# Token tiles of 128 rows, two features to a bank, two gate jobs first, and other figures in the plan of a hybrid decoder layer

## The chip, the cores and the metric

The kernel runs on one core of a Trainium2 chip. The metric is the device time of one execution in microseconds (us), the median of several runs.

## What is computed

One inference step of one layer of a hybrid decoder, for a prompt of 16 meta tokens and 512 tokens and for 8 sampled sequences of one token each; together they are T = 536 token columns of D_MODEL = 1024 features, all in fp32.

```python
h = rmsnorm(x, norm_mix)
(qa, ka, va, za, ba, aa, qb, kb, vb, rb, lrb, gate_a, gate_b) = split(h @ w_in)
qkv_a = silu(causal_dwconv(concat(qa, ka, va)))       # then l2norm of q and k
o_a, s_a = gated_delta_net(qa, ka, va, g_a, beta_a)   # chunks for the prompt, recurrent for samples
o_b, s_b = gla(qb, kb, vb, lg_b)
o_a = rmsnorm(o_a, onorm_a) * silu(za)
o_b = rmsnorm(o_b, onorm_b) * silu(rb)
mix = sigmoid(gate_a) * (o_a @ w_a_out) + sigmoid(gate_b) * (o_b @ w_b_out)
x = x + mix @ w_o
h = rmsnorm(x, norm_ffn)
u, gf = split(h @ w_ffn_in)
x = x + (gelu(causal_dwconv(u) + b) * gf) @ w_ffn_out
y = rmsnorm(x, norm_final)
```

The states of both recurrences and of both convolutions are outputs as well.

## The kernel before

**Jobs.** Activations lie transposed: 128 features on the partitions, the 536 token columns along the free axis. A job computes 128 output features for a range of columns: for each of 8 feature blocks of 128 (4 or 22 in some), three matmuls of fp32r parts (`wh` with the high part of the activations, `wh` with the low part, `wl` with the high part), each in two halves of the columns, into one of two PSUM buffers `g`. So a job with 8 blocks is 48 matmuls. The weights of a block pair are loaded as `wr`; ScalarE casts them to `wh`, VectorE takes the rest `wl` (GpSimd for the first two jobs). After the last matmul an evacuation function reads `g`.

**Order of the jobs** (`one`, line 1720 on): `z0` to `z3` (the gate of the delta net); the convolution jobs `dj` 4 and 5; the small job (beta, decay, low rank); `dj` 6, 7, 0 to 3, 8 to 11; `kb`, `qb`, `rb`, `vb`; 16 gate jobs (`ga` and `gb`, stored in `z_d`); then `w_a_out` and `w_b_out` in turn, `w_o`, and the FFN. The first nine jobs read the tokens scaled by `norm_mix` only (`xh`, `xl`, from `xact`) and their evacuation multiplies by the row `rx` of inverse norms. The others read the normalised `hTh`, `hTl` (`hact`). `z0` and `z1` form a group that does the first half of the columns of both before the second half of both, so that work can begin with half of the tokens.

**The prologue.** `loads` brings the tokens as `xu`. TensorE first runs 28 fp32 warm-up products (two instructions each). `turn` then transposes: before, tile 4 (16 meta tokens) with tiles 0 and 1 for the first half, tiles 2 and 3 with 8 sampled tokens for the second, feature block by feature block, each into its own PSUM bank (`s`, four banks). ScalarE writes `xh` from the bank, VectorE `xl`, and the raw copy `xr` is made by VectorE and ScalarE in turn. `token_norms` squares each tile on ScalarE, raises to the power -0.5 on GpSimd, has VectorE make a diagonal matrix `dg`, and TensorE multiplies ones with it to spread the norms over all partitions as `rx`. `normalised` then makes `hn`, `hTh`, `hTl` per feature block, and stores `xr` to DRAM as `xT_d` for the residual.

**The recurrences.** `gdn_prep`, `gdn_chain` and the `onorm` of key a work on the delta net once its convolutions are done; `gla_decay`, `gla_prep` (which sets a flag `gat0` to `gat4` after each chunk; `gat0` are the meta tokens), `gla_chain`, `gla_sample` and the `onorm` of key b work on GLA. `gla_sample` loads the eight states `Sg` and reads them with small matmuls (`reads`) that add up in one `s` bank; it waits for `gat4`. All of this is issued beside the jobs.

**The order of instructions** is decided in Python before the program is built. Class `Plan` collects every operation with a priority (its time in a rough model less a lead, set by `ahead`), simulates the engines, the DMA queue and the buffers with a cost per operation, and emits the instructions in the order that the simulation gives. The costs stand in `Engine.__getattr__` (from line 366), `mm` and `tr` (from line 414); `Plan.emit` holds the model of the DMA queue (`bw`) and of latencies. On the chip each engine then takes its instructions in that order.

Of the kernel before, what the change touches and what calls it, by code (L numbers as in the profile page):

```python
# [78 lines left out]


# [37 lines left out]
class Plan:  # L118
# [50 lines left out]
    def emit(self):  # L169
# [38 lines left out]
        while len(done) < len(ops):  # L208
# [54 lines left out]
            for u in op.users:  # L263
                u.left -= 1
                u.need = max(u.need, op.finish - (op.lat if op.eng == u.eng == "PE" else 0.0))
                if u.left == 0:
                    offer(u)
# [92 lines left out]
class Engine:  # L360
# [5 lines left out]
    def __getattr__(self, name):  # L366
        f = getattr(self.eng, name)

        def call(*args, **kw):
# [24 lines left out]
def body(ctx, tc, I, O):  # L394
# [19 lines left out]
    def mm(out, lhsT, rhs, start=True, stop=True):  # L414
        n, m = rhs.shape[-1], lhsT.shape[-1]
        k = lhsT.shape[0]
        small = rhs.dtype != F32R and (m <= 64 or k <= 64)
        if rhs.dtype == F32R:
            cost = max(n / 2400 + .0117, .112 * m / P, .025)
        else:  # L420
            cost = n / 2400 + .005 if m <= 32 or k <= 32 else .058 if m <= 64 and n <= 64 else max(n / 600 + .005, .222 * m / P)
        duty = (n / 2400 if rhs.dtype == F32R else n / 2400 + .007 if m <= 32 else n / 600) * k / P
        drv.matmul(cost, out, [lhsT, rhs], lambda: nc.tensor.matmul(out=out, lhsT=lhsT, rhs=rhs, start=start, stop=stop), duty, small)  # L423

    def tr(out, in_):
        k = in_.shape[0]
        drv.matmul(max(.03, .110 * k / P), out, [in_], lambda: nc.tensor.transpose(out, in_, ident[:k, :k]), 2 * k / 2400 * k / P, k <= 64)  # L427
# [26 lines left out]
    def halves(c0, n):  # L454

        return (0, NMETA + 2 * P - c0), (NMETA + 2 * P - c0, n)
# [41 lines left out]
    def load_raw(src, K, lead=12.0):  # L498
        raw = drv.new("wr", 3, pp.tile([P, 8, P], F32, tag="wr", name="wr", bufs=3))
        with ahead(lead):  # L500
            dma(out=raw[:, :K, :], in_=src.rearrange("(k p) m -> p k m", p=P))
        return raw
# [12 lines left out]
    class Weights:  # L515
# [6 lines left out]
        def first(self, *leads):  # L522

            for lead in leads:
                s, K, j = self.q[self.nr]
                self.raw[self.nr] = load_raw(s, K, drv.t + lead)
                self.nr += 1

        def ahead(self, nr, nw, eng=None):
            while self.nr < min(self.i + nr, len(self.q)):  # L530
                s, K, j = self.q[self.nr]
                self.raw[self.nr] = j.loaded() if j.loaded else load_raw(s, K)
# [100 lines left out]
    def R_(name, dt=F32R):  # L633
# [16 lines left out]
    pool.memset(half, -0.5)  # L650

    W_LEADS = 25.0, 24.0
    loads = [(cst[:, C_ID:C_ID + P], I["cst"][:, C_ID:C_ID + P]), (xts[0][0], I["x_prompt"][0, 0:P, :]),
             (nmr, I["norm_mix"][0].rearrange("(k p) -> k p", p=P)), (xts[4][0], I["meta_tokens"]),
             (xts[1][0], I["x_prompt"][0, P:2 * P, :]), None, None,
             (xts[2][0], I["x_prompt"][0, 2 * P:3 * P, :]), (xts[3][0], I["x_prompt"][0, 3 * P:4 * P, :]),
             (xts[5][0], I["x_sample"][:, 0, :]), (xu[2][NMETA:NMETA + NS, :DM], I["x_sample"][:, 0, :]), (cst[:, P:], I["cst"][:, P:])]
    for n, l in enumerate(loads):
        if l:
            with ahead(30.0 - n):  # L660
                dma(out=l[0], in_=l[1])

# [11 lines left out]
    def turn(tiles, c0, c1):  # L674

        for k in range(8):
            ps = S_()
            for i in tiles:
                xt, c = xts[i]
                tr(ps[:, c - c0:c - c0 + xt.shape[0]], xt[:, k * P:(k + 1) * P])  # L680
            x, hi, lo = (t[k // 4][:, k % 4, c0:c1] for t in (xr, xh, xl))
            pv = ps[:, :c1 - c0]
            act.activation(hi, pv, AF.Copy, scale=nrm_mix[:, k:k + 1])
            stt(lo, pv, nrm_mix[:, k:k + 1], f32(hi), MUL, SUB)
            if k % 2:
                act.copy(x, pv)
            else:
                dve.tensor_copy(x, pv)

    def token_norms(tiles):  # L690

        for i in tiles:

            xt, n = (xts[i][0], P) if i < 4 else (xu[2][:NMETA + NS, :DM], NMETA + NS)
            r = rsx[:n, i:i + 1]
            act.activation(T_("jk")[:n], xt, AF.Square, scale=DM ** -0.5, accum_out=ssx[:n, i:i + 1])
            pool.tensor_scalar_add(r, ssx[:n, i:i + 1], EPS)
            tt(r, r, half[:n], ALU.pow, pool)
            dg = Cc("dg")[:n, :n]
            dve.tensor_scalar_mul(dg, ident[:n, :n], r)  # L700
            ps = S_()
            mm(ps[:, :n], cst[:n, C_SEL + R_ONE:C_SEL + R_ONE + 1].to_broadcast([n, P]), dg)
            for a, b, c in [(0, P, xts[i][1])] if i < 4 else [(0, NMETA, 0), (NMETA, n, TP)]:
                dve.tensor_copy(rx[:, c:c + b - a], ps[:, a:b])

    def normalised():
        for i in range(2):
            dma(out=xT_d[:, 4 * i:4 * i + 4, :], in_=xr[i])
        for k in range(8):
            h = Cc("hn")[:, :T]  # L710
# [56 lines left out]
    def small_evac(ps):  # L767
        sv = Cc("sv")[:96, :T]
        tt(sv, ps, rx[:96], MUL)
# [588 lines left out]
    def gla_sample():  # L1358

        yield from drv.wait("D", "kb3", "qb3", "gdns", "gat4")  # L1360
# [70 lines left out]
    def z_evac(n, norms=None):  # L1431
        def f(ps):
            zt = Z_("zt")[:, :TQ]
            if norms is not None:
                tt(zt, ps, norms[:, Q0:T], MUL)
                act.activation(zt, zt, AF.Silu)
# [283 lines left out]
    one = [wj(OFF_ZA + n * P, Q0, TQ, z_evac(n, rx), acts=xact, halves=n < 2) for n in range(4)]  # L1720
    one += [dj(4, rx, acts=xact), dj(5, rx, acts=xact), Job([(None, 8)], xact, 0, T, small_evac, M=96, loaded=small_raw)]
    one += [dj(m, rx, acts=xact) for m in (6, 7)] + [dj(m) for m in (0, 1, 2, 3, 8, 9, 10, 11)]
# [4 lines left out]
    one += [wj(OFF_GA + n * P, Q0, TQ, z_evac(12 + n)) for n in range(16)]  # L1727
# [98 lines left out]
```

## Time and profile before

| | us |
|---|---|
| median of 3 runs (lowest to highest) | 986.65 (986.44 to 990.56) |
| profiled execution | 986.13 |
| its span | 984.4 |
| TensorE busy | 968.4 (98%) |
| VectorE busy | 606.6 (62%) |
| ScalarE busy | 463.3 (47%) |
| GpSimd busy | 185.3 (19%) |

In the rows PE is TensorE's matmul part and PEld its weight load, DVE is VectorE, ACT is ScalarE, POOL is GpSimd, SP is the engine that issues the DMAs. L389, L423 and L427 are the lines of helpers (every vector operation, every matmul, every transpose), so operations are told apart by the tiles: `out<-in`. Matmuls are pipelined: the distance from one start to the next is what one costs, not its own duration.

### The profile page before, as it was taken

How to read it: one execution, taken by the hardware profiler on the slowest of the kernel's cores; microseconds unless marked ns; L12 is line 12 of the kernel's file. 1: busy time of each engine (PE TensorE's matmuls, PEld its weight loads, DVE VectorE, ACT ScalarE, POOL GpSimd, SP SyncE). 2: the span in 40 equal slices, each digit the busy share in tenths (PEclk: the TensorE clock that was granted, in tenths of full speed). 3: DMA queues.
4: the chain of work that ended last, by engine and by line, in shares of the span. 5: the costliest groups of instructions: out<-in, count | busy, mean ns of one | idle time of the engine just before them, and what ended most of it. 6: DMA issues, size and time to landing. Idle time of an engine off the chain costs nothing.

```text
span 984.4 us, 21968 instructions
## 1 busy us (share of the span) xinstructions
PE 968.4 (98%) x9022; PEld 950.4 (97%) x9022; DVE 606.6 (62%) x1197; ACT 463.3 (47%) x905; POOL 185.3 (19%) x278
## 2 busy tenths in 40 slices
PE   9999999999999999999999999999999999999996
PEld 8999999998999999999999999999999999999996
DVE  4879867883457867324754447777776766433254
ACT  6566654745446455244643337344443433232343
POOL 4100116101222244012211122111122111000000
PEclk9999999999999999999999999999999999999998
DMA  7643322445123232656655536477655554433354
GB/s 235 184 116 88 87 66 65 133 130 142 34 77 87 79 90 83 188 161 204 204 174 150 162 110 182 139 237 213 199 157 156 166 152 126 126 118 93 111 143 140
DMA packets 208681, 135.48 MB, mean 138 GB/s; under 512 B 14353, under 2 KB 196392, under 8 KB 208308
## 3 DMA queue, kind: packets, MB, share of 16 engines
q1 hardware_dynamic: 208580, 134.07, 46.9%
q8 instruction: 71, 1.16, 0.5%
q14 instruction: 30, 0.25, 0.1%
HBM read 112.26 MB, written 21.98 MB: 136 GB/s over the span
## 4 chain that ended last, share of the span: by engine, by line
PE 81%; DMA 1%; issue 0%; DVE 0%; ACT 0%; SPq 0%; POOLq 0%; POOL 0%; ACTq 0%
PE g L423 71%; PE s L423 8%; PE s L427 1%; DMA xb_d<-Xb 0%; DMA NT<-xb_d 0%; PE on L423 0%; ACT zt L389 0%; PE pk L423 0%; SPq L389 0%; PE pq L423 0%; POOLq L1822 0%; ACT gat L389 0%; DVE wy L389 0%; DVE ga L389 0%; POOL rfb L389 0%
## 5 line engine op out<-in xcount | busy, mean ns | idle before, releaser
L389 ACT CAST wh<-wr 128x512 fp32r<-128x512 f32 (+1 forms) x300 | 183.1, 612 | 312.3 <-PE g L423 297.4
L389 DVE TENSOR_TENSOR wl<-wr,wh 128x512 fp32r<-128x512 f32 (+1 forms) x296 | 203.6, 698 | 177.1 <-ACT wh L389 175.4
L423 PE MATMUL g<-hTh,wh 128*128 128x268 f32 (+3 forms) x768 | 160.8, 288 | 1.0 <-ACT zt L389 1.0
L423 PE MATMUL g<-hTl,wh 128*128 128x268 f32 (+3 forms) x768 | 161.7, 288 | 0.0
L423 PE MATMUL g<-hTh,wl 128*128 128x268 f32 (+3 forms) x768 | 160.9, 288 | 0.0
L423 PE MATMUL g<-h2l,wh 128*128 128x260 f32 x704 | 142.8, 284 | 0.0
L423 PE MATMUL g<-h2h,wh 128*128 128x260 f32 x704 | 142.0, 282 | 0.0
L423 PE MATMUL g<-h2h,wl 128*128 128x260 f32 x704 | 142.0, 283 | 0.0
L423 PEld LDWEIGHTS g<-hTh,wh 128*128 128x128 f32 x768 | 120.0, 189 | 3.6 <-issue 1.9
L423 PEld LDWEIGHTS g<-hTl,wh 128*128 128x128 f32 x768 | 120.9, 189 | 1.7 <-issue 1.2
L423 PEld LDWEIGHTS g<-hTh,wl 128*128 128x128 f32 x768 | 119.8, 189 | 1.5 <-issue 1.2
L423 PEld LDWEIGHTS g<-h2h,wl 128*128 128x128 f32 x704 | 109.3, 189 | 0.1
L423 PEld LDWEIGHTS g<-h2h,wh 128*128 128x128 f32 x704 | 108.6, 189 | 0.1
L423 PEld LDWEIGHTS g<-h2l,wh 128*128 128x128 f32 x704 | 108.6, 189 | 0.0
L423 PE MATMUL g<-actl,wh 128*128 128x260 f32 (+2 forms) x352 | 79.3, 284 | 0.0
L423 PE MATMUL g<-acth,wh 128*128 128x260 f32 (+2 forms) x352 | 78.2, 283 | 0.0
L423 PE MATMUL g<-acth,wl 128*128 128x260 f32 (+2 forms) x352 | 77.9, 282 | 0.0
L423 PEld LDWEIGHTS g<-actl,wh 128*128 128x128 f32 x352 | 57.7, 188 | 0.1
L423 PEld LDWEIGHTS g<-acth,wl 128*128 128x128 f32 x352 | 57.3, 188 | 0.0
L423 PEld LDWEIGHTS g<-acth,wh 128*128 128x128 f32 x352 | 57.2, 188 | 0.0
L389 ACT ACT_TABLE_LOAD x34 | 43.6, 1283 | 7.4 <-DVE na L389 3.4
L389 POOL TENSOR_TENSOR E<-kb,E 128x256 f32<-128x256 f32 (+1 forms) x32 | 25.5, 807 | 56.5 <-DVE E L389 31.9
(362 smaller groups left out, 1675.5 us busy)
## 6 DMA issues: line engine op xcount, KB each, us to landing
wr<-in_w_in SPq DMA_DIRECT2D x56, 512.0 KB
wr<-in_w_ffn_in SPq DMA_DIRECT2D x44, 512.0 KB
wr<-in_w_ffn_out SPq DMA_DIRECT2D x20, 512.0 KB
z_d<-zt SPq DMA_DIRECT2D x28, 261.0 KB
Sg<-in_state_gla SPq DMA_DIRECT2D x8, 512.0 KB
wr<-in_w_b_out SPq DMA_DIRECT2D x8, 512.0 KB
wr<-in_w_o SPq DMA_DIRECT2D x8, 512.0 KB
So<-in_state_gla SPq DMA_DIRECT2D x8, 512.0 KB
```

The lines of the kernel that those rows point to most:

```text
L389: self.drv.issue(self.key, cost, out, ins, 2.2 if self.key == "sync" else 0.17, lambda: f(*args, **kw), func, lock)
L423: drv.matmul(cost, out, [lhsT, rhs], lambda: nc.tensor.matmul(out=out, lhsT=lhsT, rhs=rhs, start=start, stop=stop), duty, small)
L427: drv.matmul(max(.03, .110 * k / P), out, [in_], lambda: nc.tensor.transpose(out, in_, ident[:k, :k]), 2 * k / 2400 * k / P, k <= 64)
```

## The change

Tokens are tiled by 128 rows from the first meta token on: five tiles, the last of 16 prompt tokens and 8 samples, and the halves are cut at column 256 (`XH`). `turn` puts `per` feature blocks into a bank, two in the first half and one in the second; in the second half (and for the last bank of the first) ScalarE makes `xr`. `token_norms` works on groups of tiles (0, 1 and 2, 3, 4), squares odd tiles on VectorE, and multiplies the column of norms, spread along the free axis, with the identity instead of ones with a diagonal. `xT_d` is stored block by block. `z0` and `z1` run over all 536 columns. Two gate jobs come fifth and sixth, on `xact`, with `rx` in their evacuation; `dj` 4 to 7 and the small job read `hact`, so their evacuations multiply by no norm. `gla_sample` waits for `gat1`. In the plan, an operation that follows another on the same engine waits for less of its latency (`saved`), the DMA queue starts at 2.8 us and moves 320 instead of 300 (thousand bytes per us), and small matmuls and transposes cost other amounts.

```diff
+    def saved(self, user):
+
+        return 0.0 if user.eng != self.eng or self.eng == "sync" else self.lat - (0.0 if self.eng == "PE" else 0.03)
...
-        self.free, self.hw, self.bw, self.queue, self.set = {}, 0.0, 0.0, [], None
+        self.free, self.hw, self.bw, self.queue, self.set = {}, 0.0, 2.8, [], None
...
-                    op.need = max(op.need, d.finish - (d.lat if d.eng == op.eng == "PE" else 0.0))
+                    op.need = max(op.need, d.finish - d.saved(op))
...
-                cost = n * out[0].shape[0] * max(4 / 300e3, 0.43e-3 / run)
+                cost = n * out[0].shape[0] * max(4 / 320e3, 0.43e-3 / run)
...
-            cost = n / 2400 + .005 if m <= 32 or k <= 32 else .058 if m <= 64 and n <= 64 else max(n / 600 + .005, .222 * m / P)
+            cost = n / 2400 + .005 if m <= 32 else .12 if m <= 64 and n <= 64 else max(n / 600 + .005, .222 * m / P if k > 32 else 0.0)
...
-        drv.matmul(max(.03, .110 * k / P), out, [in_], lambda: nc.tensor.transpose(out, in_, ident[:k, :k]), 2 * k / 2400 * k / P, k <= 64)
+        drv.matmul(max(.05, .110 * k / P), out, [in_], lambda: nc.tensor.transpose(out, in_, ident[:k, :k]), 2 * k / 2400 * k / P, k <= 64)
...
-        return (0, NMETA + 2 * P - c0), (NMETA + 2 * P - c0, n)
+        return (0, XH - c0), (XH - c0, n)
...
-    xts = [(xu[i // 2][:, (i % 2) * DM:(i % 2 + 1) * DM], NMETA + i * P) for i in range(4)]
-    xts += [(xu[2][:NMETA, :DM], 0), (xu[2][:NS, DM:2 * DM], TP)]
-    XH = NMETA + 2 * P
+    xts = [xu[i // 2][:, (i % 2) * DM:(i % 2 + 1) * DM] for i in range(4)] + [xu[2][:T - 4 * P, :DM]]
+    XH = 2 * P
...
+    def turn(tiles, c0, c1, per):
+
+
+        for k0 in range(0, 8, per):
+            ps = S_()[:, :per * (c1 - c0)].rearrange("p (k t) -> p k t", k=per)
+            for k in range(k0, k0 + per):
+                for i in tiles:
+                    n = xts[i].shape[0]
+                    tr(ps[:, k - k0, i * P - c0:i * P - c0 + n], xts[i][:, k * P:(k + 1) * P])
+            for k in range(k0, k0 + per):
+                hi, lo = (t[k // 4][:, k % 4, c0:c1] for t in (xh, xl))
+                act.activation(hi, ps[:, k - k0], AF.Copy, scale=nrm_mix[:, k:k + 1])
+                stt(lo, ps[:, k - k0], nrm_mix[:, k:k + 1], f32(hi), MUL, SUB)
+            x = xr[k0 // 4][:, k0 % 4:k0 % 4 + per, c0:c1]
+            with ahead(16.0):
+                if per == 1 or k0 == 6:
+                    act.copy(x, ps)
+                else:
+                    dve.tensor_copy(x, ps)
+
+    def token_norms(tiles):
+
+        a, b = tiles[0], tiles[-1] + 1
+        for i in tiles:
+            n = xts[i].shape[0]
+            jk, ss = T_("jk")[:n], ssx[:n, i:i + 1]
+            if i % 2:
+                dve.scalar_tensor_tensor(out=jk, in0=xts[i], scalar=1.0 / DM, in1=xts[i], op0=MUL, op1=MUL, accum_out=ss)
+            else:
+                act.activation(jk, xts[i], AF.Square, scale=DM ** -0.5, accum_out=ss)
+        pool.tensor_scalar_add(rsx[:, a:b], ssx[:, a:b], EPS)
+        tt(rsx[:, a:b], rsx[:, a:b], half.to_broadcast([P, b - a]), ALU.pow, pool)
+        ps, c = S_(), a * P
+        for i in tiles:
+            n = xts[i].shape[0]
+            mm(ps[:, i * P - c:i * P - c + n], rsx[:n, i:i + 1].to_broadcast([n, P]), ident[:n, :n])
+        n = min(b * P, T) - c
+        dve.tensor_copy(rx[:, c:c + n], ps[:, :n])
...
-        for i in range(2):
-            dma(out=xT_d[:, 4 * i:4 * i + 4, :], in_=xr[i])
         for k in range(8):
+            dma(out=xT_d[:, k, :], in_=xr[k // 4][:, k % 4, :])
...
-        yield from drv.wait("D", "kb3", "qb3", "gdns", "gat4")
+        yield from drv.wait("D", "kb3", "qb3", "gdns", "gat1")
...
-    one += [dj(4, rx, acts=xact), dj(5, rx, acts=xact), Job([(None, 8)], xact, 0, T, small_evac, M=96, loaded=small_raw)]
-    one += [dj(m, rx, acts=xact) for m in (6, 7)] + [dj(m) for m in (0, 1, 2, 3, 8, 9, 10, 11)]
+    one = [wj(OFF_ZA + n * P, 0 if n < 2 else Q0, T if n < 2 else TQ, z_evac(n, rx), acts=xact, halves=n < 2) for n in range(4)]
+    gate_job = lambda n, norms=None, **kw: wj(OFF_GA + n * P, Q0, TQ, z_evac(12 + n, norms), **kw)
+    one += [gate_job(n, rx, acts=xact) for n in range(2)]
+    ng = 2
+    raw_, own = dict(norms=rx, acts=xact), ()
+    one += [dj(m, **(raw_ if m in own else {})) for m in (4, 5)]
+    one.append(Job([(None, 8)], xact if 's' in own else hact, 0, T, small_evac, M=96, loaded=small_raw))
...
-    one += [wj(OFF_GA + n * P, Q0, TQ, z_evac(12 + n)) for n in range(16)]
+    one += [gate_job(n) for n in range(ng, 16)]
...
-        turn((4, 0, 1), 0, XH)
+        turn((0, 1), 0, XH, 2)
...
-        turn((2, 3, 5), XH, T)
-    with ahead(20.0):
-        token_norms((0, 1, 2, 3, 4))
+        turn((2, 3, 4), XH, T, 1)
+    with ahead(18.0):
+        token_norms((0, 1))
+        token_norms((2, 3, 4))
```

## Rows read from the trace of the kernel before

**Rows 1.** The page: busy times, the chain that ended last, the weight split.

```profile
PE 968.4 (98%) x9022; PEld 950.4 (97%) x9022; DVE 606.6 (62%) x1197; ACT 463.3 (47%) x905; POOL 185.3 (19%) x278
...
PE 81%; DMA 1%; issue 0%; DVE 0%; ACT 0%; SPq 0%; POOLq 0%; POOL 0%; ACTq 0%
...
L389 DVE TENSOR_TENSOR wl<-wr,wh 128x512 fp32r<-128x512 f32 (+1 forms) x296 | 203.6, 698 | 177.1 <-ACT wh L389 175.4
```

**Rows 2.** TensorE's waits: who was waited for, us in total, times, longest.

```profile
PE s L427 <- DVE xr L389: 0.8, 1, 0.8
...
PE g L423 <- DVE zt L389: 0.4, 1, 0.4
```

**Rows 3.** Instructions of the warm-up: duration ns min/median/max, first and last start.

```profile
L423 PE MATMUL warm<-scm x56: 275/275/579, 1.3 to 10.9; 128*128 128x128 f32 x56
```

**Rows 4.** Windows of the start: length, busy (count) per engine, clock, DMA share, GB/s.

```profile
0.00:11.00 11.00, 9.45 (x67) 8.97 (x67) 1.83 (x6) 5.84 (x10) 5.57 (x18) 1.00 0.83 252
...
11.00:31.47 20.47, 19.65 (x160) 18.09 (x160) 14.75 (x38) 16.14 (x36) 8.44 (x16) 1.00 0.74 243
...
31.50:57.00 25.50, 25.14 (x207) 24.96 (x206) 21.53 (x39) 12.22 (x24) 2.90 (x9) 1.00 0.51 130
```

**Rows 5.** TensorE's timeline in the prologue: start us, us, instruction, count.

```profile
11.49 0.88 PE L427 MATMUL s<-cst,xu 16*128 16x16 f32 x6
12.13 0.36 PE L423 MATMUL g<-xh,wh 128*128 128x258 f32 x1
...
15.74 0.38 PE L427 MATMUL s<-cst,xu 128*128 128x128 f32 x2
15.88 0.36 PE L423 MATMUL g<-xl,wh 128*128 128x258 f32 x1
16.08 0.29 PE L423 MATMUL g<-xh,wl 128*128 128x258 f32 x1
```

**Rows 6.** Windows of one 522-wide job, and of two that are 536 wide.

```profile
37.77:43.64 5.87, 5.87 (x48) 5.87 (x49) 4.57 (x7) 3.38 (x7) 0.00 (x0) 1.00 0.63 144
43.64:55.52 11.88, 11.88 (x99) 11.88 (x98) 10.70 (x19) 4.88 (x9) 1.76 (x5) 1.00 0.44 135
```

**Rows 7.** Instructions of the tiles `xr` and `jk` (the squares) on ScalarE.

```profile
L389 ACT COPY xr<-s x8: 378/384/386, 11.2 to 27.0; 128x272 f32<-128x272 f32 x4, 128x264 f32<-128x264 f32 x4
...
L389 ACT ACTIVATE jk<-xu x5: 1054/1058/1082, 5.2 to 25.9; 128x1024 f32<-128x1024 f32 x4, 24x1024 f32<-24x1024 f32 x1
L389 ACT ACTIVATION_READ_ACCUMULATOR jk<-xu x5: 184/187/224, 6.2 to 26.9; 128x1 f32 x4, 24x1 f32 x1
```

**Rows 8.** Instructions of the tiles `hn`, `hTl`, `zt` and `xT_d`.

```profile
L389 DVE SCALAR_TENSOR_TENSOR hn<-xr,vec,rx x8: 767/770/777, 32.5 to 62.9; 128x536 f32<-128x536 f32 x8
L389 DVE TENSOR_TENSOR hTl<-hn,hTh x8: 708/712/718, 35.6 to 69.0; 128x536 fp32r<-128x536 f32 x8
...
L389 DVE TENSOR_TENSOR zt<-g,rx x4: 693/701/704, 29.9 to 46.8; 128x522 f32<-128x522 f32 x4
...
L389 SPq DMA_DIRECT2D xT_d<-xr x2: 332/345/358, 22.2 to 27.4; - x2
```

**Rows 9.** Instructions of the tiles `Sg`, `ob` and `olb`: the GLA line.

```profile
L423 PE MATMUL s<-Sg,zw x64: 379/379/403, 405.4 to 432.9; 128*32 128x256 f32 x64
L389 DVE SCALAR_TENSOR_TENSOR Sg<-Sg,edl,s x16: 471/476/481, 359.6 to 404.0; 128x256 f32<-128x256 f32 x16
...
L389 ACT ACTIVATE osq<-ob x8: 622/630/646, 435.8 to 442.5; 128x522 f32<-128x522 f32 x8
...
L389 DVE TENSOR_TENSOR olb<-zl,ohb x8: 690/703/1564, 465.4 to 485.9; 128x522 fp32r<-128x522 f32 x8
```

**Rows 10.** Windows of the recurrences, and the stretch below full clock.

```profile
200.00:300.00 100.00, 98.18 (x1203) 94.56 (x1202) 56.12 (x138) 48.81 (x81) 17.18 (x26) 0.98 0.35 95
300.00:400.00 100.00, 98.61 (x1362) 94.80 (x1361) 73.58 (x163) 49.51 (x100) 36.89 (x42) 1.00 0.29 84
...
250.00:260.00 10.00, 10.00 (x103) 9.80 (x102) 4.66 (x14) 4.43 (x7) 1.04 (x1) 0.83 0.27 81
```

More of the change, by code (lines that the diff above doesn't have):

```diff
@@ L264, in emit @@
                 u.left -= 1
-                u.need = max(u.need, op.finish - (op.lat if op.eng == u.eng == "PE" else 0.0))
+                u.need = max(u.need, op.finish - op.saved(u))
                 if u.left == 0:
@@ L496, in patient, with load_raw @@
         drv.hold = hold
-    def load_raw(src, K, lead=12.0):
+    def load_raw(src, K, *leads):
         raw = drv.new("wr", 3, pp.tile([P, 8, P], F32, tag="wr", name="wr", bufs=3))
-        with ahead(lead):
-            dma(out=raw[:, :K, :], in_=src.rearrange("(k p) m -> p k m", p=P))
+        n = K // len(leads)
+        for i, lead in enumerate(leads):
+            with ahead(lead):
+                dma(out=raw[:, i * n:(i + 1) * n, :], in_=src[i * n * P:(i + 1) * n * P].rearrange("(k p) m -> p k m", p=P))
         return raw
@@ L522, in first @@
         def first(self, *leads):
-            for lead in leads:
+            for l in leads:
                 s, K, j = self.q[self.nr]
-                self.raw[self.nr] = load_raw(s, K, drv.t + lead)
+                self.raw[self.nr] = load_raw(s, K, *l)
                 self.nr += 1
@@ L650, in body @@
     pool.memset(half, -0.5)
[L652 to L657, printed above, removed]
+    pool.memset(ssx, 1.0)
+    x_p = I["x_prompt"][0]
+    loads = [(cst[:, C_ID:C_ID + P], I["cst"][:, C_ID:C_ID + P]),
+             (nmr, I["norm_mix"][0].rearrange("(k p) -> k p", p=P)),
+             (xts[0][:NMETA], I["meta_tokens"]), (xts[0][NMETA:], x_p[0:P - NMETA]),
+             (xts[1], x_p[1 * P - NMETA:2 * P - NMETA]),
+             None,
+             None,
+             (xts[2], x_p[2 * P - NMETA:3 * P - NMETA]),
+             (xts[3], x_p[3 * P - NMETA:4 * P - NMETA]),
+             (xts[4][:NMETA], x_p[SEQ - NMETA:]), (xts[4][NMETA:], I["x_sample"][:, 0, :])]
+    W_LEADS = [[30.0 - n] for n, l in enumerate(loads) if not l]
     for n, l in enumerate(loads):
@@ L661, in body @@
                 dma(out=l[0], in_=l[1])
+    with ahead(4.0):
+        dma(out=cst[:, P:], in_=I["cst"][:, P:])
     def warm_up():
@@ L672, in turn_weights @@
         dve.tensor_copy(nrm_mix, ps[:, :8])
-    def turn(tiles, c0, c1):
-        for k in range(8):
[L677 to L704, printed above, removed]
@@ L710, in normalised @@
+    def normalised():
+        for k in range(8):
+            dma(out=xT_d[:, k, :], in_=xr[k // 4][:, k % 4, :])
             h = Cc("hn")[:, :T]
@@ L1434, in f @@
             if norms is not None:
-                tt(zt, ps, norms[:, Q0:T], MUL)
-                act.activation(zt, zt, AF.Silu)
+                tt(zt, ps[:, ps.shape[-1] - TQ:], norms[:, Q0:T], MUL)
+                if n < 12:
+                    act.activation(zt, zt, AF.Silu)
             elif n < 12:
@@ L1718, in body @@
     xact = lambda k: (xh[k // 4][:, k % 4, :], xl[k // 4][:, k % 4, :])
-    one = [wj(OFF_ZA + n * P, Q0, TQ, z_evac(n, rx), acts=xact, halves=n < 2) for n in range(4)]
-    one += [dj(4, rx, acts=xact), dj(5, rx, acts=xact), Job([(None, 8)], xact, 0, T, small_evac, M=96, loaded=small_raw)]
-    one += [dj(m, rx, acts=xact) for m in (6, 7)] + [dj(m) for m in (0, 1, 2, 3, 8, 9, 10, 11)]
+    one = [wj(OFF_ZA + n * P, 0 if n < 2 else Q0, T if n < 2 else TQ, z_evac(n, rx), acts=xact, halves=n < 2) for n in range(4)]
[5 more added lines that the diff above has]
+    one.append(Job([(None, 8)], xact if 's' in own else hact, 0, T, small_evac, M=96, loaded=small_raw))
+    for i, m in enumerate((6, 7, 0, 1, 2, 3, 8, 9, 10, 11)):
+        if i in ():
+            one.append(gate_job(ng))
+            ng += 1
+        one.append(dj(m, **(raw_ if m in own else {})))
     one += [wj(OFF_KB + h * P, 0, T, qkb_evac(kb, h, 1.0, f"kb{h}")) for h in range(H)]
```

6 lines of the change are left out of this document (2 added, 4 removed).

## The prediction

> **What bounds the kernel now.** I read the page first: TensorE is busy for 98% of the span and the chain that ended last is almost all PE [rows 1]. Then TensorE's own waits, stage by stage: the largest one after the start is a 0.8 us wait of a transpose for the copy `xr`, then 0.4 us for `zt` [rows 2]. So no other engine is a bound. The span is the sum of what TensorE issues, and a change moves the time only where it takes instructions off TensorE, makes them cheaper, or opens or closes a wait there. The start is full as well: 56 warm-up matmuls run from 1.3 to 10.9 us [rows 3], and the two windows of the prologue are idle for 1.55 us (1.3 of them before the first matmul) and for 0.82 us, at a granted clock of 1.00 [rows 4]. The first weight matmul therefore waits for queued warm-ups and transposes rather than for data, and a transpose saved there is worth its issue time.
>
> The span is 984.4 us, the profiled execution took 986.13 us, the median of the runs is 986.65 us. I work in differences and set them against the median; the 0.5 us between execution and median is within the spread of the runs.
>
> **Part by part.**
>
> *Tiles of 128 rows.* Before, each of 8 features has a 16-row transpose in the first half and an 8-row one in the second; after, only the second half has a small one (24 rows). Eight transposes go. Price: six transposes of two features (four of 128 rows, two of 16) hold the next weight matmul from 11.49 to 12.13, 0.64 us; a pair of 128-row ones takes 15.74 to 15.88, 0.14 us [rows 5]. So the two small ones with their change of shape cost 0.64 - 2 x 0.14 = 0.36, or 0.18 each: 8 x 0.18 = **-1.44 us**. The 24-row tile has the bound of 0.18 too and replaces the 8-row one at no difference.
>
> *Two features to a bank.* The matmul after a run of transposes needs 0.20 us to the next (15.88 to 16.08) [rows 5], where a job of 48 pairs of weight and token columns takes 5.87 us [rows 6], 0.12 us each: 0.08 us a turn. The first half turns 4 times for 8: **-0.32 us**.
>
> *Wait for the bank.* The 0.8 us [rows 2] is a transpose of the second half that waits until VectorE has copied `xr` out. After, the first half needs half as many banks, and in the second half ScalarE does the copies. ScalarE is not fuller for it: it was busy 16.14 of 20.47 us there [rows 4]; it keeps eight copies of 0.38 us and gets one of 512 columns (some 0.7 us, an estimate from 0.38 us for 264 to 272), and gives up one of the three squares that it did in this stretch, 1.06 + 0.19 us [rows 7]. VectorE takes that square and loses its five `dg` and five of its eight copies. I take **-0.8 us**; the ends are -0.8 and +0.8 (the same wait, once more, behind a ScalarE that now does scale and copy in turn).
>
> *Wider first jobs.* `z0` and `z1` run over 536 columns for 522. Two 536-wide jobs take 11.88 us, a 522-wide one 5.87 us [rows 6]: 0.07 us a job, **+0.14 us**.
>
> *Norm rows without diagonals.* Still five small matmuls; `dg` leaves VectorE, where it was not on the path. 0; the row `rx` is done earlier, which `normalised` needs.
>
> *Two gate jobs first.* The same 16 jobs in another place: 0 on TensorE as long as three covers hold. (a) `dj4` to `dj7` and the small job now read the normalised `hT`, so it is needed after six raw jobs, not nine. With the prologue over 2.4 us earlier, at 29.1, and four jobs of 5.87, `dj4` starts at 52.6 and its last feature is wanted 7/8 x 5.94 later, at 57.8. Between 29.1 and 57.8 VectorE must do 8 x (0.77 + 0.71) for `hT`, 6 x 0.70 for `zt` [rows 8] and the weight splits of six jobs, 12 x 0.70 [rows 1]: 24.5 of 28.7 us, 85%. It showed 21.53 of 25.5 us, 84%, in just that stretch [rows 4]. So it fits with nothing to spare, unless `rx` comes sooner: 0, up to +9.5 (below). (b) The stores of `xT_d` go from two to eight, 0.35 us of issue each [rows 8]; they stand on SP ahead of weight loads, but SP no longer holds them back until half of `xr` is there: 0. The two gate stores use the one `zt` buffer; the wait seen there was 0.4 us [rows 2], the upper end for each, +0.8 in all. (c) The convolutions end two jobs later, 11.7 us, less 2.4, so GDN and GLA start 9.3 us later while the jobs that need them do not move.
>
> *Reads at chunk two.* These give (c) its cover. Before, the last state update of the GLA chain starts at 404.0, then the sample reads run 405.4 to 432.9, and only at 435.8 do the squares of its norm begin; its last product is at 485.9 + 0.7 [rows 9]. With the reads beside the chain some 30 us of that line go, and 9.3 are spent. The reads stay as many: 64 instructions. They may run in more pieces (one more change of shape each, up to eight at the 0.18 above, +1.4) or join other small work (-1.4); I take 0. They hold one of four `s` banks meanwhile; the weight jobs fill that.
>
> *Figures of the plan.* New costs order everything after the prologue anew. What could be won there is what is lost now: 1.82 and 1.39 us of idle between 200 and 400 us, and 1.7 us of half clock in 250 to 260 (10 x (1 - 0.83)) [rows 10], together 4.9 us. As much could be lost again. Nothing in the trace says which; I take 0 with both ends.
>
> Sum: -1.44 - 0.32 - 0.8 + 0.14 = -2.4 us. **986.65 - 2.4 = 984.2 us.**
>
> **The rivals.**
>
> *The order recovers the losses* (26%): latencies between instructions of one engine are believed shorter, small matmuls dearer, so the order holds better. For it: TensorE takes its instructions in the order of the plan, so an idle there is an order that came out wrong. Against: it is idle for only 3.2 of 200 us there [rows 10], and a new order can err anew. It gives 984.2 - 4.9 = 979.3 us.
>
> *`hT` late*, the one that ends slower (8%): TensorE stands before `dj4`. Before, the eighth `hTl` started at 69.0 although the first `hn` ran at 32.5 [rows 8]; nothing needed it sooner. If it keeps that pace and starts 2.4 us earlier it is there at 67.3, against 57.8: a stall of 9.5 us, 993.7 us. Below a stall of 2.4 us it is no loss; from 7.3 us on it is slower by over 0.5%. For it: the 85% above. Against: `hn` can start as soon as `rx` and one `xr` stand, and VectorE was idle for 5.7 of the 20.47 us of the prologue [rows 4].
>
> *The GLA norm late* (6%): were the reads still done last, the squares would start 9.3 us after 435.8 and the norm end at 495.9, where TensorE now wants it at 486.6 - 2.4: 11.7 us, 995.9 us. Against: the new flag is set three of the four full chunks earlier. For it: the reads take their buffers in turn with the chain's states.
>
> *A slow clock at the start* (10%). In this trace the prologue with its 48 transposes (8 blocks of six tiles) runs at 1.00 [rows 4], and the one stretch below it, in 250 to 260 us [rows 10], is where small matmuls crowd. After, up to 16 transposes stand together. If the clock fell once, as there, that is 1.7 us: 985.9 us. The Trainium skill speaks for this rival ("TensorE: Matmul & The Clock Gate", Part 4: PE-mode transpose): there a transpose does not count as activity for the clock gate. By that rule the packed transposes would be the place to fall; the trace, at 1.00 with transposes among matmuls, does not bear it out so far.
>
> **How the numbers follow.** The forecast, 984.2 us, has 50%; the rivals 26, 8, 6 and 10%. A measurement of this kernel can tell about 0.5%, 4.9 us, from no change. The forecast and the slow clock lie within it: 60% same; the recovered order is faster: 26%; the two late norms slower: 14%. The range: down to the recovered order with a little of the -1.4 of the reads, 978.5; up to the forecast with the other ends of its terms (1.6 for the bank, 0.8 for the stores, 1.4 for the reads, and 2 us of a worse order), 990. It leaves out about 5% below and 12% above.
>
> **What would show it.** The prologue right: the first 262-wide matmul (`z2`) starts near 29.1, not 31.47, and no wait for `xr` is left. Eight transposes fewer on `xu`. No wait of TensorE for `hTl` or `hTh` at `dj4`, near 52.6; the last `hTl` before 57.8. The sample reads between 330 and 420, the squares of the GLA norm soon after the last state update, and no wait for `ohb`. Between 200 and 400 us idle and clock about as before. I am wrong if the gain or loss stands after 100 us: then the order, not the prologue, decided. A stall of over 2.4 us at `dj4` or at the first `w_b_out` job would make it slower.

## The result, and the profile after

The changed kernel takes **981.06 us** (median of 9 executions, 977.98 to 983.50) against 987.42 us of the kernel before (9 beside it, 984.44 to 990.59): a ratio of 0.9931, interval 0.9916 to 0.9947. It is 6.4 us or 0.7% faster. Forecast were 2.4 us, 984.2 us; the rival in which the order recovers its losses gave 979.3 us and came nearer. Where a gain in us of time is named below, it is the ratio's share of some 987 us.

The page after (answers [rows 1]): TensorE is as long busy, 968.4 us, in a span of 981.6 us.

```profile
PE 968.4 (99%) x9014; PEld 953.6 (97%) x9014; DVE 611.0 (62%) x1185; ACT 466.0 (47%) x906; POOL 185.1 (19%) x273
...
PE 94%; DVE 2%; ACT 1%; DMA 1%; issue 1%; POOL 0%; SPq 0%; POOLq 0%
```

TensorE's waits after (answers [rows 2]; who was waited for, us in total, times, longest):

```profile
PE s L427 <- issue: 1.4, 2, 1.1
PE warm L427 <- POOL scm L393: 1.3, 1, 1.3
PE g L427 <- DVE gl L393: 1.0, 1, 1.0
PE s L431 <- DVE x L393: 0.5, 1, 0.5
PE s L427 <- DMA NT<-xb_d: 0.5, 2, 0.2
PE s L427 <- DVE NT L393: 0.2, 1, 0.2
```

The waits for `xr` and `zt` are gone. Gone as well is one for `ga` (0.8 us before) that no row ahead of the prediction shows. New is one of 1.0 us for `gl`, in the feed-forward stage.

Windows after (answers [rows 4] and [rows 10]; length, busy per engine, clock, DMA share, GB/s):

```profile
11.00:31.47 20.47, 20.47 (x169) 19.46 (x168) 15.96 (x33) 17.32 (x39) 7.81 (x14) 1.00 0.76 214
200.00:300.00 100.00, 98.44 (x1239) 94.50 (x1239) 60.09 (x146) 50.19 (x81) 17.73 (x25) 0.98 0.44 119
300.00:400.00 100.00, 99.68 (x1368) 95.19 (x1368) 76.99 (x165) 52.01 (x104) 38.93 (x44) 0.97 0.34 99
355.00:360.00 5.00, 5.00 (x51) 3.89 (x51) 3.17 (x6) 2.80 (x6) 2.73 (x4) 0.50 0.02 3
```

The prologue has no idle left. Between 300 and 400 us 1.1 us of idle went, but this execution has a stretch at half clock (0.50, 1.2 GHz) that the one before had not. So two terms must be kept apart in all that follows. I give each kernel's median time, and beside it the median of span times mean granted clock, here called the **full-clock span**: an estimate of what the span would be had the clock stayed at 2.4 GHz. It is 980.7, 981.5 and 981.2 us for the kernel before in the three sets of runs below, 973.7 us for the changed one.

The estimate is rough in two places, so a difference of less than about 1 us in it tells nothing. The records of the granted clock begin only when the clock has risen, and what the first warm-ups lose at half pace is not in it. And every profile ends at half clock with TensorE idle (the kernel before, then the changed one):

```profile
977.30:984.40 7.10, 0.00 (x0) 0.00 (x0) 1.69 (x5) 1.15 (x1) 1.52 (x2) 0.50 0.41 152
```

```profile
976.00:981.60 5.60, 0.00 (x0) 0.00 (x0) 1.07 (x2) 0.72 (x1) 0.35 (x1) 0.50 0.52 193
```

That end costs nothing (from the first down job on, every profile takes 140.3 to 140.7 us), yet the estimate takes 2.0 to 3.6 us off for it.

Tiles after (answers [rows 5], [rows 7] to [rows 9]; duration ns min/median/max, first and last start in us):

```profile
L431 PE MATMUL s<-cst,xu x40: 213/272/328, 7.4 to 21.6; 128*128 128x128 f32 x32, 24*128 24x24 f32 x8
...
L393 DVE TENSOR_TENSOR hTl<-hn,hTh x8: 702/710/718, 32.4 to 52.2; 128x536 fp32r<-128x536 f32 x8
...
L427 PE MATMUL s<-Sg,zw x64: 379/379/403, 296.6 to 319.9; 128*32 128x256 f32 x64
...
L393 DVE SCALAR_TENSOR_TENSOR Sg<-Sg,edl,s x16: 471/474/480, 373.3 to 413.9; 128x256 f32<-128x256 f32 x16
...
L393 ACT ACTIVATE osq<-ob x8: 622/632/645, 407.7 to 413.5; 128x522 f32<-128x522 f32 x8
...
L393 DVE TENSOR_TENSOR olb<-zl,ohb x8: 690/692/697, 440.9 to 460.8; 128x522 fp32r<-128x522 f32 x8
```

Eight transposes fewer; `hTl` done at 52.9, where I had estimated that nothing needs its last block before 57.8; the sample reads 109 us earlier (I had said between 330 and 420), the GLA norm done at 461.5 for 486.6 before.

TensorE at the start, after, and then in the changed kernel with late reads (below), whose prologue has the same instructions (start us, us, instruction, count):

```profile
1.32 5.69 PE L427 MATMUL warm<-scm 128*128 128x128 f32 x26 [1.32 <-POOL scm L393]
...
30.02 0.41 PE L427 MATMUL g<-xh,wh 128*128 128x262 f32 x2
```

```profile
1.32 5.10 PE L427 MATMUL warm<-scm 128*128 128x128 f32 x26 [1.32 <-POOL scm L393]
...
29.45 0.41 PE L427 MATMUL g<-xh,wh 128*128 128x262 f32 x2
```

The same 26 warm-ups take 5.69 and 5.10 us: the first ones run at half pace until the clock rises, and that moment, at which the records of the granted clock begin, differs (4.53 us into the span before, 6.64 after, 5.41 in the second). Between these two kernels a rise 1.23 us later costs 0.59 us, about half of the delay, so `z2` at 30.02 for 31.47 is a prologue 1.45 us shorter, or 2.5 us at the same rise ((6.64 - 4.53) / 2 more).

### The profile page after: what moved, and what is told of

Its sections match the earlier page's. It is cut to its first block, busy times and chain, and to the rows that moved or that the text cites. A ratio compares the mean times of both kernels' runs of the same rounds, so it can differ in the third digit from the quotient of the medians.

```text
span 981.6 us, 21954 instructions
## 1 busy us (share of the span) xinstructions
PE 968.4 (99%) x9014; PEld 953.6 (97%) x9014; DVE 611.0 (62%) x1185; ACT 466.0 (47%) x906; POOL 185.1 (19%) x273
## 4 chain that ended last, share of the span: by engine, by line
PE 94%; DVE 2%; ACT 1%; DMA 1%; issue 1%; POOL 0%; SPq 0%; POOLq 0%
PE g L427 81%; PE s L427 8%; PE s L431 2%; PE warm L427 1%; DMA xb_d<-Xb 1%; DVE fy L393 0%; DMA NT<-xb_d 0%; PE pk L427 0%; PE pq L427 0%; DVE wl L393 0%; ACT L393 0%; DVE Xb L393 0%; DVE tmpb L393 0%; ACT wh L393 0%; PE pd L431 0%
## 5 line engine op out<-in xcount | busy, mean ns | idle before, releaser
L393 DVE TENSOR_TENSOR wl<-wr,wh 128x512 fp32r<-128x512 f32 (+1 forms) x296 | 206.5, 706 | 176.4 <-ACT wh L393 174.7
L427 PE MATMUL g<-hTh,wh 128*128 128x268 f32 (+4 forms) x816 | 173.2, 290 | 0.0
L427 PE MATMUL g<-hTl,wh 128*128 128x268 f32 (+4 forms) x816 | 170.9, 288 | 0.0
L427 PE MATMUL g<-hTh,wl 128*128 128x268 f32 (+4 forms) x816 | 170.4, 288 | 0.0
L427 PEld LDWEIGHTS g<-hTh,wh 128*128 128x128 f32 (+1 forms) x816 | 128.2, 189 | 1.6 <-issue 1.2
L427 PEld LDWEIGHTS g<-hTl,wh 128*128 128x128 f32 (+1 forms) x816 | 128.1, 189 | 1.4 <-issue 1.1
L427 PEld LDWEIGHTS g<-hTh,wl 128*128 128x128 f32 (+1 forms) x816 | 127.8, 189 | 0.6 <-issue 0.4
```

The source lines that it names most:

```text
L393: self.drv.issue(self.key, cost, out, ins, 2.2 if self.key == "sync" else 0.17, lambda: f(*args, **kw), func, lock)
```

## The experiments

The theory, from the windows above: the gain is the plan's new figures, and the prologue adds little. The rival is my forecast: the prologue is the gain. The first three kernels tell them apart; the second four, which figure, and whether the early gates matter; the rest, what gates and reads do with either set of figures. A third reading belongs beside both: the order of before was merely a poor draw, and any of several new orders beats it. "us" is the median; the ratio is to the kernel before, in the same set.

| kernel | us | ratio, interval | full-clock span |
|---|---|---|---|
| prologue alone | 987.07 | 1.0004, 0.9992 to 1.0017 | 979.3 (before 980.7) |
| figures alone | 979.63 | 0.9926, 0.9913 to 0.9940 | 974.0 (980.7) |
| change, old figures | 980.82 | 0.9943, 0.9924 to 0.9962 | 974.6 (980.7) |
| change, late reads | 977.45 | 0.9914, 0.9898 to 0.9930 | 973.7 (980.7) |
| `saved` alone | 982.35 | 0.9945, 0.9923 to 0.9966 | 977.0 (981.5) |
| costs alone | 985.82 | 0.9989, 0.9972 to 1.0006 | 977.7 (981.5) |
| DMA figures alone | 986.69 | 0.9985, 0.9967 to 1.0003 | 980.5 (981.5) |
| change, gates last | 981.00 | 0.9932, 0.9907 to 0.9956 | 972.9 (981.5) |
| reads alone | 983.47 | 0.9966, 0.9948 to 0.9984 | 977.1 (981.2) |
| prologue and gates | 988.15 | 1.0006, 0.9992 to 1.0020 | 981.8 (981.2) |
| prologue and figures | 979.39 | 0.9912, 0.9895 to 0.9930 | 974.1 (981.2) |
| late reads, old figures in plan two | 977.75 | 0.9891, 0.9871 to 0.9912 | 972.6 (981.2) |

**Prologue alone.** The changed kernel with the old figures, reads and job order (and the norm back in the small job's evacuation). The new prologue also loads the tokens and the norm weights in another order, which the list of the change does not name; that comes with it here.

```diff
-    ng = 2
-    raw_, own = dict(norms=rx, acts=xact), ()
+    ng = 0
+    raw_, own = dict(norms=rx, acts=xact), (4, 5, 's', 6, 7)
```

> The kernel before with the new prologue alone: tiles of 128 rows, two features to a bank, norm rows without diagonals, z0 and z1 over 536 columns; the job order, the reads at gat4 and the figures of the plan are those of before. Theory P (the prologue was priced right and the other 4 us come from elsewhere): 2.4 us faster than before (ratio 0.9976), z2 starts 2 to 3 us earlier, apart from the moment at which the clock rises at the start. Rival W (all of the 6.4 us follow from the prologue, since everything after it is ordered anew): 6 us faster (0.994).

Nothing in the time (at most 0.8 us by the interval), 1.4 us in the full-clock span. My forecast, made a kernel, brings at most what its first term said, and falls as the cause.

**Figures alone**, in the kernel before (two of the lines):

```diff
-                    op.need = max(op.need, d.finish - (d.lat if d.eng == op.eng == "PE" else 0.0))
+                    op.need = max(op.need, d.finish - d.saved(op))
...
+            cost = n / 2400 + .005 if m <= 32 else .12 if m <= 64 and n <= 64 else max(n / 600 + .005, .222 * m / P if k > 32 else 0.0)
```

> The kernel before with the new figures of the plan alone (latency on the same engine, DMA start and rate, costs of small matmuls and transposes). Theory F (the figures give a better order in the recurrences): 3 to 4.5 us faster than before (ratio about 0.996), the idle of TensorE between 150 and 500 us falls from 4.4 us to about 2 us, and the span times the granted clock falls by as much. Rival G (the gain outside the prologue comes from the early gate jobs or the early reads): within 1 us of before.

7.3 us, all of the change's gain and more than the 3 to 4.5 that I expected. The stretch from the last product of `z1`, one before the first 262-wide one, to the first `w_a_out` one, and from there to the first `w_o` one, in the kernel before and then with the figures alone (windows as above):

```profile
31.35:470.05 438.70, 434.78 (x4603) 419.94 (x4602) 288.54 (x622) 231.43 (x412) 93.34 (x136) 1.00 0.39 109
470.05:540.89 70.84, 70.05 (x580) 69.84 (x579) 40.54 (x60) 30.30 (x53) 15.70 (x11) 1.00 0.59 177
```

```profile
31.55:463.20 431.65, 430.82 (x4605) 417.98 (x4604) 293.24 (x634) 237.88 (x420) 94.73 (x139) 1.00 0.41 114
463.20:532.66 69.46, 69.46 (x578) 69.46 (x577) 31.44 (x48) 26.92 (x46) 13.07 (x9) 1.00 0.55 164
...
PE g L428 <- DVE gl L394: 0.9, 1, 0.9
```

The first stretch is 7.05 us shorter: idle falls from 3.92 to 0.83, and TensorE is busy 3.96 us less for the same number of products. Of these 1.7 us are the half clock in 250 to 260 [rows 10], which is not there in this execution. That the figures remove it is not shown: the changed kernel has the same figures and again shows 0.83 in 250 to 260, and of the eight profiles with `saved` or the new costs four have such a stretch between 200 and 400 us, of the six without both all six. The other 2.25 us stand in no wait, only in shorter distances between instructions. Fewer changes of shape they are not (counted from one product to the next in this stretch: 236 before, 243 with the figures); they stay open. The second is 1.4 us shorter, 0.8 of it the wait for `ga`. The feed-forward stage pays 0.9 us back, waiting for `gl`.

**The change with the old figures:**

```diff
-                    op.need = max(op.need, d.finish - d.saved(op))
+                    op.need = max(op.need, d.finish - (d.lat if d.eng == op.eng == "PE" else 0.0))
```

(and the other five lines back).

> The changed kernel with the old figures of the plan: the other side of the run before. Theory F: about 2.4 us faster than before, 4 us slower than the changed kernel (ratio about 0.9975). Rival G: as the changed kernel, 6 us faster (0.9935). If it is slower than before, the new parts need the new figures.

So the parts do not add: without the figures the change still gains 5.6 us, nearer to rival G, though its prologue alone gains nothing. It does not gain them in quite the same places:

```profile
29.97:466.21 436.24, 433.04 (x4605) 419.88 (x4604) 298.31 (x632) 235.25 (x421) 98.41 (x143) 1.00 0.43 118
466.21:535.85 69.64, 69.64 (x578) 69.64 (x577) 30.03 (x46) 24.21 (x41) 11.46 (x7) 1.00 0.49 148
...
PE s L427 <- DMA NT<-xb_d: 1.3, 1, 1.3
PE g L427 <- ACT zt L393: 1.0, 2, 0.7
...
PE g L427 <- DVE zt L393: 0.6, 1, 0.6
```

The start is 1.4 us shorter, the first stretch 2.5 and the second, where the wait for `ga` is gone, 1.2; the waits for `zt` and `NT`, which the figures alone remove or cut, stay.

**Which figure.** `saved` alone, the costs of `mm` and `tr` alone, the DMA queue alone (for this last one, with 320 for 300):

```diff
-        self.free, self.hw, self.bw, self.queue, self.set = {}, 0.0, 0.0, [], None
+        self.free, self.hw, self.bw, self.queue, self.set = {}, 0.0, 2.8, [], None
```

> The kernel before with one figure alone: an operation that follows another on its own engine waits for 0.03 us of its latency instead of 0.17 (TensorE for none, as before). Of the figures together 7.2 us were measured. Theory S (VectorE and ScalarE are ordered better, so buffers of the weight jobs come free in time): 5 us or more faster (ratio 0.995 or less) and the waits of TensorE for zt and ga, 1.0 and 0.8 us before, are gone. Rival C (the dearer small matmuls keep TensorE from changing between shapes and from running dry): within 1.5 us of before.

> The kernel before with the new costs of small matmuls and transposes alone. Theory S: within 2 us of before. Rival C: 4 us or more faster; fewer changes of shape and no stretch at half clock in 200 to 300 us.

> The kernel before with the new DMA figures alone (queue starts at 2.8 us, 320 instead of 300). All theories: within 1.5 us of before, a little at the start, since no wait of TensorE for a load is left but 0.2 us. If it is 4 us or more faster by itself like the others, any new order gains, and the order of before was merely a bad draw.

`saved` carries the largest part, 4.5 us of full-clock span and 5.4 of time; with it ScalarE's `zt` and the `NT` loads are no longer waited for, but `ga` still is, against the expectation (TensorE's waits with `saved` alone; the first stretch with `saved`, then with the costs):

```profile
PE g L428 <- DVE ga L394: 0.8, 1, 0.8
PE s L432 <- ACT vb L394: 0.6, 1, 0.6
...
PE g L428 <- DVE zt L394: 0.4, 1, 0.4
PE s L428 <- DVE NT L394: 0.2, 1, 0.2
```

```profile
32.02:465.74 433.72, 432.42 (x4604) 418.12 (x4603) 289.62 (x622) 233.92 (x414) 92.78 (x136) 1.00 0.40 111
```

```profile
32.24:466.79 434.55, 432.25 (x4606) 418.20 (x4605) 289.04 (x630) 234.31 (x416) 94.62 (x138) 1.00 0.41 113
```

The first stretch is 5.0 and 4.2 us shorter than before; without the 1.7 us of half clock, which neither profile has, these are 3.3 and 2.4 us, and 5.3 with all figures. The costs shorten the full-clock span by 3.8 us, but these runs spent more at half clock and their time can't be told from none; the profile is of the fastest of their twelve. The queue's figures bring 1.0 us or nothing. Alone they sum to 9.3 us for 6.7 together.

**Gates last**, in the changed kernel (the diff under "prologue alone", the rest as changed), and **late reads**:

```diff
-        yield from drv.wait("D", "kb3", "qb3", "gdns", "gat1")
+        yield from drv.wait("D", "kb3", "qb3", "gdns", "gat4")
```

> The changed kernel with the two gate jobs back at the end, and dj4 to dj7 and the small job back on the raw tokens with the norm in their evacuation. Gate theory (the early gates shift the recurrences under other jobs and win there): 3 us slower than the changed kernel. Theory F (order comes from the figures, the gates give nothing): within 1.5 us of the changed kernel, full-clock span 973.7 plus or minus 1.

> The changed kernel with the sample reads back behind the last chunk of the GLA preparation (gat4). My cover argument: the GLA norm then ends about 11.7 us after the moment at which the first w_b_out job wants it, so TensorE stands there for up to 11 us and the time is 3 to 5 us above before. Rival L (the norm line of before was stretched by priorities and can be done faster): no wait of TensorE for ohb, within 1.5 us of the changed kernel. Rival R (the early reads give the gain outside the prologue): 4 us slower than the changed kernel, with no wait for ohb, but more changes of shape on TensorE.

With the new figures neither the place of two gate jobs nor the early reads gains: 972.9 and 973.7 us of full-clock span for 973.7. Late reads are not late for the norm either; `w_b_out` starts without a wait. The time even falls with them, by 0.17% here and 0.20% between "gates last" and "prologue and figures", which differ by the reads alone. Each pair lies within its intervals, and neither full-clock span shows a loss by the early reads (973.7 in both; 972.9 with them, 974.1 without); so early reads may cost 2 us through the clock, and it is not shown.

**Reads alone** (the flag `gat1` for `gat4`, in the kernel before), and **prologue and gates** (the changed kernel with the old figures and late reads):

> The kernel before with one edit: the sample rows of the GLA output are released at the second chunk instead of the fifth. Prologue, gate jobs and figures are the old ones. It asks whether the early reads carry the 4.7 us (full-clock span 979.3 to 974.6) by which the change with the old figures beats its prologue alone. Theory A, the reads are work moved inside a stage that the tensor engine fills, and bring nothing by themselves: 985 to 988, ratio 0.998 to 1.002, full-clock span 979.5 to 981.5, idle of the tensor engine from the first full-width z job to the first w_a_out still 3 to 5 us. Theory B, the early reads take their short matmuls out of the late part of the stage, where the losses of the old order stand: 981 to 983, ratio 0.994 to 0.996, full-clock span 975 to 977, idle there under 2 us. Theory C, each edit deals the order anew and a loss of the old order may go with any of them: a full-clock span anywhere between 976 and 983, with the waits of the old order (for zt, NT, ga) replaced by others.

> The changed kernel with the old figures in the plan's model and the sample reads of the GLA output at the fifth chunk: the new prologue and the two early gate jobs, and nothing else. Beside the prologue alone (ratio 1.0004, full-clock span 979.3) it shows the gate jobs with the old figures, and beside the change with the old figures (0.9943, 974.6) the reads. Theory A, the gate jobs are only moved: 986 to 988, ratio 0.999 to 1.002, full-clock span 978.5 to 980. Theory B, the gate jobs carry what the prologue alone gave back in the middle: 980 to 983, ratio 0.993 to 0.996, full-clock span 974 to 976, idle from the first full-width z job to the first w_a_out near 3 us instead of 5.5. The start is the same in both: the first full-width z job 29.5 to 30.5 us from the start of the span.

Here the reads do gain: 3.4 us alone. In the profile the two stretches are:

```profile
30.33:468.05 437.72, 433.09 (x4606) 419.87 (x4604) 298.30 (x636) 235.43 (x422) 96.67 (x140) 1.00 0.41 115
468.05:537.51 69.46, 69.46 (x578) 69.46 (x577) 30.03 (x46) 23.30 (x40) 11.45 (x7) 1.00 0.49 145
```

The idle of the first is not less than before (4.63 for 3.92 us), so theory B has nearly the time but not the cause; the second is 1.4 us shorter, without the wait for `ga`. And the early gates need the reads. With the gates early, the reads late and the old figures, the stretch of `w_a_out` and `w_b_out` is 74.84 us instead of 70.83 (prologue alone), for this (window; waits; tile):

```profile
467.31:542.15 74.84, 72.70 (x587) 71.14 (x586) 43.99 (x71) 32.32 (x57) 21.01 (x15) 1.00 0.61 181
...
PE g L427 <- ACT ohb L393: 1.6, 2, 0.9
...
L393 DVE TENSOR_TENSOR olb<-zl,ohb x8: 691/704/1096, 474.8 to 490.3; 128x522 fp32r<-128x522 f32 x8
```

This is the rival of the late GLA norm: `olb` ends at 491.0, and TensorE stands for the first `ohb` from 474.0 on. The stage is 4.0 us longer where I priced 11.7; 1.35 us of that are idle, the rest is busy time that I did not divide. With the early reads added (the change with old figures) the stretch is 69.64 us and the wait gone. So the last part of the change does give the gate jobs the cover that I named, but only an order made with the old figures needs it.

**Prologue and figures** (the changed kernel with both diffs above, gates last and late reads):

> The changed kernel without two of its parts: the gate jobs stand last again, and the sample reads of the GLA output are released at the fifth chunk. What is left is the new prologue and the new figures. If these two are the whole of the gain: 976.5 to 979.5, ratio 0.990 to 0.993, full-clock span 972.5 to 974.5. If the early gate jobs or the early reads carry a part of it: 981 to 985, ratio 0.9945 to 0.998, full-clock span over 975.5. If prologue and figures add in full (2.5 and 7.2 us): 976 to 977.

0.9912 against 0.9926 of the figures alone: the prologue's 1.4 us would be just this, and the intervals overlap. The full-clock spans, 7.1 and 6.7 us below their own before, say 0.4. In the profile the prologue is shorter, but 1.1 us of idle stand later, for a load of `Sg` and for `zc`.

**Old figures in the second plan**, with late reads:

```diff
+OLDF = []
...
+        if OLDF:
+            return self.lat if self.eng == user.eng == "PE" else 0.0
...
+    OLDF.append(1)
     drv.add(ffn_norm())
```

> The changed kernel with the sample reads at the fifth chunk, and with the old figures in the second of the two plans, the one that orders the feed-forward stage; the first plan keeps the new figures. It tests whether the new figures cost 0.9 to 1.0 us in the feed-forward stage (a wait of the tensor engine for the vector engine's gl there). If they do: the wait is gone, the stage from the first gate-and-up job to the first down job takes 255.0 instead of 256.0 us, full-clock span 972.5 to 973.2 for 973.7, the time 975.5 to 977.5, ratio 0.9900 to 0.9915. If the wait comes from how the first plan ends: stage 256.0 again, 977 to 978.5, ratio 0.991 to 0.993.

The feed-forward stage of the changed kernel with late reads, and then of this one:

```profile
579.27:835.33 256.06, 255.11 (x2121) 254.82 (x2120) 187.06 (x337) 111.83 (x229) 50.06 (x88) 1.00 0.57 167
```

```profile
582.29:837.32 255.03, 255.03 (x2121) 254.83 (x2120) 185.78 (x337) 111.76 (x229) 50.24 (x88) 1.00 0.57 168
```

1.03 us of stage, 0.95 of it idle, and 1.1 us of full-clock span. It is the best ratio here, 0.9891, though its interval overlaps that of late reads alone.

**What the runs show together.** Every kernel with `saved` or with the early reads is faster (ratios 0.9891 to 0.9966), and none of the four with neither can be told from before in the time (0.9985 to 1.0006). Each of the two gains by itself, and together they gain no more than `saved` with the other figures. So the order after the prologue makes the gain, and that is shown. Why these two edits deal the better order is shown only for the waits named; that the order of before was a poor draw, which unlike edits happen to improve, is not excluded.

## Why the prediction came out as it did

*What bounds the kernel: right, but read in part.* TensorE's instructions and waits set the time in every kernel here. I named two of its waits, though, and took the one for `xr` as the largest. Beside them stood these, of the kernel before:

```profile
PE g L423 <- ACT zt L389: 1.0, 2, 0.7
PE s L423 <- issue: 1.0, 1, 1.0
PE s L423 <- DMA NT<-xb_d: 0.8, 2, 0.5
PE g L423 <- DVE ga L389: 0.8, 1, 0.8
...
PE s L423 <- DVE atd L389: 0.4, 1, 0.4
```

These are 4.0 us in the middle, and all but the one of issue are of a kind that another order can remove.

*The failed step: "Figures of the plan ... Nothing in the trace says which; I take 0".* Measured alone: -6.7 us of full-clock span, -7.3 us of time. Of the losses I listed, 3.2 us of idle and 1.7 of half clock, the idle was the right one: between `z2` and `w_a_out` the figures took 3.1 us of it, and beyond it 2.25 us that no idle shows and 1.4 us in the stage after, and gave 0.9 back for `gl`. The half clock is absent from that profile, but the changed kernel has it again. So 4.9 us was short by a third, but the error was to call the term undecided. The trace did speak on it, in the waits above: each but the one of issue is an instruction that the plan had put ahead of a result that was not there yet, and `saved` alone takes those for ScalarE's `zt` and for the `NT` loads away. That the plan had believed these results earlier is not shown; no run compares its times with the chip's.

*Tiles and turns, -1.44 and -0.32: right in place, smaller in the time.* Eight transposes went, `z2` starts 1.45 us earlier, 2.5 at the same rise of the clock, which is the -2.4 of the sum. Over the profiles `z2` starts at 30.35 to 32.36 us with the old prologue (six) and at 29.45 to 30.32 with the new one (eight). What failed is that this start would reach the end: alone the prologue leaves 1.4 us in the full-clock span and none in the time. In that execution idle between `z2` and `w_a_out` gave a part back, 5.55 us instead of 3.92; 1.4 of the 1.6 are the wait put down to issue (2.4 for 1.0 us), whose cause is not shown, and three stretches at half clock there (one before) took 3.4 us more.

*Wait for the bank, -0.8: about right on average, its cause further back than I read.* The kernel with the reads alone issues the start of the kernel before, instruction for instruction, and has no such wait. VectorE's and TensorE's rows of the kernel before, then VectorE's of that one:

```profile
18.39 1.08 DVE L389 CAST gkR<-gkr 16x512 fp32r<-16x512 f32 x1 [1.79 <-DMA gkr<-in_w_gk]
...
20.27 0.44 PE L427 MATMUL s<-cst,xu 128*128 128x128 f32 x2 [0.78 <-DVE xr L389]
```

```profile
17.79 0.44 DVE L389 CAST gkR<-gkr 16x512 fp32r<-16x512 f32 x1 [1.17 <-DMA gkr<-in_w_gk]
...
18.56 0.41 DVE L389 COPY xr<-s 128x264 f32<-128x264 f32 x1
```

VectorE stood before the cast of `gkR` for a load; `xl` and `xr` were queued behind it. The load came 1.79, 1.17 and, with the figures alone, 3.25 us after VectorE was ready; TensorE's wait was 0.8, 0 and 1.2 us. So in the kernel before, how long the wait is depends on when that load comes, and the term is 0 to -1.2, by the execution. Over the profiles the wait for `xr` is there in four of six with the old prologue (0.8, 1.2, 0.8, 1.2 us, 0.67 on average over the six) and in none of eight with the new one. Where ScalarE makes the copies of the second half, VectorE still stands for that load (0.93 us in the changed kernel) and TensorE no longer waits.

*Wider jobs, norm rows, gates first: 0 and 0.14, held.* The last `hTl` ends at 52.9, `dj4` reads `hTh` from 53.31 on without a wait; the rival of the late `hT` (slower) did not occur. VectorE was busy for 19.53 of 23.40 us from 29.5 to 52.9, 83% where I had 85%, with four `zt` and nine `wl` between; `hn` started at 29.8 instead of 32.5.

*Reads at chunk two, 0 with -1.4 and +1.4: too narrow.* With the old figures they are worth 3.4 us of time alone and 6.2 between "prologue and gates" and the change with old figures; with the new ones nothing.

*The slow clock at the start: not there.* From 11 us on the prologue is at 1.00, with up to seven transposes in a run (nine before that). The 1.00 that I read for 0 to 11 us says nothing of the first warm-ups, since the records begin only at the rise. Nor is 250 to 260 the one stretch below full clock: the end is one too, with TensorE idle. In the changed kernel the clock fell at 354.8 us; TensorE had been busy without a pause, with small products (56 of 64 columns, twice 8 of 16 rows) between weight products from 350 on. The prediction cited the Trainium skill ("TensorE: Matmul & The Clock Gate", Part 4: PE-mode transpose), by which transpose mode does not count as PE-busy in the same way; the prologue's 1.00 shows no cost of it here.

*The sum.* "I am wrong if the gain stands after 100 us": it does. The time lay in the range, since the range reached to the rival. That is luck for the sum, whose terms bring nothing measurable in the time by themselves; 50% for it and 60% for no change were too many, the rival's 26% too few.

## What to carry to other kernels

Where an order is computed from a cost model, list every wait of the bounding engine, not the largest: each may be an error of the model, and a change to the model's figures should be priced by which of them it addresses. Several parts of a change may remove the same losses; add them only after trying each alone and all but each. Profile the kernel before more than once before a wait of under 1 us becomes a term.

## What the runs showed of the hardware that was not expected

- Executions of one kernel differ by how much of them runs at half clock. The changed kernel's nine go from 977.98 us at a mean granted clock of 0.997 to 983.50 at 0.992; times the clock their spans agree within 2.5 us (972.9 to 975.4).
- Every profile ends at 0.50 with TensorE idle (976.0 to 981.6 us in the changed kernel), and the last stage is not longer for it: 140.3 to 140.7 us with 2.0 to 3.6 us of clock lost there. The mean granted clock of a span counts this stretch too, though it costs nothing.
- The clock's rise at the start is not fixed to the work: 4.2 to 7.4 us into the span in the fourteen profiles, with warm-ups running from 1.32 us in each. The Trainium skill ("TensorE: Matmul & The Clock Gate", Part 1) states that one kernel starts with different counts of slow matmuls; over these profiles they are 12 to 26.
- The load of `w_gk2` at the start let its cast begin at 18.39 us in one profile and at 17.79 in another with the same order of issue up to there, and VectorE, which takes its instructions in order, passed this on to TensorE.
